# Turning the final recurrence states beside the prompt's scores, and storing the recurrence outputs later in ScalarE's order

## The chip, the cores and the metric

The kernel runs on one core of one Trainium2 chip. The metric is device time in microseconds (us) of that core for one launch. The profiled execution is a separate one with its own time. TensorE is called PE, ScalarE ACT, VectorE DVE, GpSimd POOL; SP is the engine whose queue issues nearly all the DMAs.

## The reference, cut to what matters

One layer of a hybrid backbone over 1024 latent tokens and 128 prompt tokens, width 1024, float32 (products are made exact enough by splitting an operand into a high and a low part, three matmuls for one). In the layer's mixer, one projection feeds attention heads, a gated linear recurrence and a Fourier mixing:

```
xc = dw_conv(xr, conv_w, conv_b)
hf, hf_fin = rg_lru_dir(xc, ..., h0[:, 0], False)   # forward scan
hb, hb_fin = rg_lru_dir(xc, ..., h0[:, 1], True)    # backward scan
lru_out = (hf + hb) * gelu(gr)                      # into the output projection
new_h = stack([hf_fin, hb_fin])                     # final states of the PROMPT, an output (2 x 256)
```

The prompt attends to itself only (128 x 128 scores for 4 heads x 2 maps); the latent tokens attend to themselves and a cached context. The change touches the place where `lru_out` is split and stored, and the place where `new_h` is turned from columns into rows and written out.

## The kernel before, in words

All instructions are issued in an order written out by hand; each engine runs its own in that order, and a DMA waits in SP's queue behind the DMAs ahead of it. The stretch that matters goes from 213 to 350 us of the span:

- **Projection units.** Fourteen 128-column units of the input projection (u0 and u1 during the start, then twelve in a loop over `i`), each 8 k-steps of 9 matmuls (`pu`). After each k-step `tick(1.44)` advances a planner's clock; each planner queue then runs its generator up to that clock. A generator's `yield x` asks to be resumed x later (plain `yield`: the queue's own wait, 0.806 for the four recurrence queues).
- **Recurrence queues** `ql`: two scan generators (one for each direction), one for the gates (`g` matmuls on PE, sigmoids on ACT, L581 and L583), one for the outputs, `lru_outs`. The recurrence has two halves of 128 channels, called channel half 0 and 1 here. `lru_outs` adds the two directions on POOL (L625), multiplies by the gelu gate on DVE (L628, tile `a`), waits by the `yield` that the change edits, and then runs `store_mix` in four parts: high part on ACT (L168; `mh` for half 0, `mor` for half 1), low part on DVE (L174; `ml`, `moi`), two DMAs to `MH` and `ML`.
- **Values, first half.** Nine tiles of 24 matmuls (`v`), with `tick(1.045)` twice for each tile. Their weights are loaded and split before (`load_v(0)`); `load_v(1)` loads `vr` for the second half at the end of the unit loop, splits it into `vwh` on ACT and `vwl` on DVE. Rope of the last query unit (`ry`, `rz`, `ryh`, `ryl`) runs beside it and is written to `QH`, `QL`, `QHP`, `QLP`.
- **`drain_lru()`** then empties the recurrence queues. Last in `lru_outs` before the change is the turn of the states: PE transposes `nh` (L636) into an `aux` PSUM bank ("a"), ACT copies it into a corner of `lw`, SP writes `new_h` (L640).
- **Prompt and values, second half.** `play(PRE)` interleaves, by hand, steps of `prompt_gen` ("p") with k-steps of the second half of the values ("v36" is 36 k-steps of 3 matmuls, using the two `aux` banks in turn, "a" first):

```
    PRE = "p v36 p r p p v6 v4 p v5 l v3 p"
```

  The first "p" issues the six loads of `kp` and `qp`; the second one the sixteen prompt score matmuls (`sp`, L1143, into banks 0 and 1 of a three-bank tile); at "r" the recurrence's memory is released; the third "p" issues `load_q(0, 0)` (four loads `qs`) and `load_head(0)` (two loads `ks`, then `ck`, `av`), which the first scores of the latent tokens need (`s`, L940). Attention then runs to about 525 us, the output projection and the feed-forward part follow.

Of the kernel before, what the change touches and what calls it, by code (L numbers as in the profile page):

```python
# [16 lines left out]
P = 128  # L17
# [135 lines left out]
def _body(tc, nc, A):  # L153
    PE, ACT, DVE, POOL, SP = nc.tensor, nc.scalar, nc.vector, nc.gpsimd, nc.sync
# [6 lines left out]
    def rdma(eng, out, in_):  # L161

        f = lambda v: v.bitcast(F32) if v.dtype == F32R else v
        eng.dma_start(f(out), f(in_))

    def copy(eng, out, in_):
        if eng is ACT:
            ACT.activation(out, in_, AF.Copy)  # L168
        else:
            eng.tensor_copy(out, in_)  # L170
# [31 lines left out]
    ident = cp.tile([P, P], F32, name="ident")  # L202
# [19 lines left out]
    def aux(name, tag):  # L222
        return ax.tile([P, 512], F32, name=name, tag="aux" + tag)
# [212 lines left out]
    def store_mix(stage, k, src, parts=3, full=None):  # L436

        w = T // parts
        for q in range(parts):
            c = slice(q * w, (q + 1) * w)  # L440
            if full is None:
                mh, ml = [stage.tile([P, w], F32R, name=f"m{i}{k}{q}", tag=f"m{i}", bufs=1)
                          for i in "hl"]
            else:
                mh, ml = [x[:, c] for x in full]
            copy(ACT, mh, src[:, c])
            yield
            lo(ml, src[:, c], mh)
            yield
            rdma(SP, MH[k * P:(k + 1) * P, c], mh)  # L450
            rdma(SP, ML[k * P:(k + 1) * P, c], ml)
            yield
            yield
# [94 lines left out]
    xin, ggr, lru = {}, {}, {}  # L548

    def until(*names):  # L550
        while not all(n in lru for n in names):
            yield 0.3
# [66 lines left out]
    def lru_outs(f, lw, nh):  # L619
        for u in range(2):  # L620
            yield from until(("scan", u, 0), ("scan", u, 1))
            yield 2.021
            h, h1 = lru["scan", u, 0][0], lru["scan", u, 1][0]
            o = lru["scan", u, 1][1]
            POOL.tensor_tensor(h, h, h1, op=OP.add)  # L625
            yield 2.64
            for s0, o0, w in ((0, 0, NL), (NL + GAP, NL, NP)):
                DVE.tensor_tensor(o[:, o0:o0 + w], h[:, s0:s0 + w], ggr[u][:, o0:o0 + w],  # L628
                                  op=OP.mult)
            yield 0.994  # L630
            full = ([f.tile([P, TL], F32R, name=f"mo{i}", tag=i, bufs=2) for i in "ri"] if u else None)
            yield from store_mix(f, 4 + u, o, 4, full)
            lru["out", u] = True
        yield from until(*[("fin", u, d) for u in range(2) for d in range(2)])
        b = aux("nht", "a")
        PE.transpose(b[0:4, 0:P], nh.rearrange("p d u -> p (d u)"), ident)  # L636
        yield 4.0
        nhs = lw[0:4, 0, 0, 0]
        copy(ACT, nhs, b[0:4, 0:P])
        SP.dma_start(A["new_h"].rearrange("d (u p) -> (d u) p", p=P), nhs)  # L640


    kq = {}
# [193 lines left out]
    def load_q(h, c):  # L837
        q = kv.tile([P, 2, 2, CW], F32R, name=f"qs{h}{c}", tag="qs", bufs=2)
        hs = slice(h * P, (h + 1) * P)
        for half, (s0, s1) in ((0, (QH, QL)), (1, (QL, QH))):  # L840
            ps_ = slice(64 * half, 64 * half + 64)
            for st_, src in ((0, s0), (1, s1)):
                s = src[hs].rearrange("(m d) t -> d m t", m=2)
                w = min(CW, NL - c * CW)
                rdma(SP, q[ps_, st_, :, :w], s[:, :, c * CW:c * CW + w])
        qsl[h, c] = q
# [62 lines left out]
    def aux_free(name):  # L909

        return aux(name, "ab"[((vdone - 1) // KT + 1) % 2])
# [215 lines left out]
    def prompt_gen():  # L1127

        big = lambda name, tag, dt=F32: aw.tile([P, 9 * P], dt, name=name, tag=tag,
                                                bufs=3 if tag == "wt" else 2)  # L1130
        small = lambda name, w: aw.tile([P, w], F32, name=name, tag=name, bufs=1)
        f = P_["kq"]
        kp, *qp = [f.tile([P, T], F32R, name=n, tag=t, bufs=1)
                   for n, t in (("kp", "ab0"), ("qp0", "ab1"), ("qp1", "rope"))]
        g8 = lambda x: x[:, :8 * P].rearrange("p (g c) -> p g c", c=P)
        for half, ss in ((0, (KHP, QHP, QLP)), (1, (KLP, QLP, QHP))):
            for dst, src in zip((kp, *qp), ss):
                rdma(SP, g8(dst)[64 * half:64 * half + 64], src)
        yield
        b = sc.tile([P, 3, 512], F32, name="sp", tag="s")  # L1140
        for g in range(8):
            for st_ in range(2):
                PE.matmul(b[:, g // 4, g % 4 * P:g % 4 * P + P], g8(qp[st_])[:, g], g8(kp)[:, g],  # L1143
                          start=(st_ == 0), stop=(st_ == 1))
        yield
        nm, ss, c, so = small("nmp", 8), small("ssp", 8), small("cp", 4), small("sop", 4)
        ACT.activation(ss, mhalf[:, :8], AF.Exp)
        load_q(0, 0)
        load_head(0)
        vp = aw.tile([P, CW], F32, name="vp", tag="wth", bufs=6)  # L1150
        SP.dma_start(vp[:, :2 * P], VS[NL:T, 0:2 * P])
        s = b[:, 0:2].rearrange("p a (q c) -> p (a q) c", c=P)
        DVE.tensor_reduce(nm, s, axis=AX.X, op=OP.max, negate=True)
        e = big("ep", "p0")
        for i in range(2):
            yield
            for g in range(4 * i, 4 * i + 4):
                ACT.activation(g8(e)[:, g], s[:, g], AF.Exp, bias=nm[:, g:g + 1],
                               accum_out=ss[:, g:g + 1])
        s0, s1 = ss[:, 0:8:2], ss[:, 1:8:2]  # L1160
        DVE.reciprocal(c, s1)
        DVE.scalar_tensor_tensor(c, c, nlam, s0, op0=OP.mult, op1=OP.mult)
        w, o = big("wtp", "wt"), big("op", "wt")
        hd = lambda x, h: x[:, h * P:(h + 1) * P]
        for h in range(NH):
            DVE.scalar_tensor_tensor(hd(w, h), g8(e)[:, 2 * h + 1], c[:, h:h + 1], g8(e)[:, 2 * h],
                                     op0=OP.mult, op1=OP.add)
        yield
        b = aux_free("tpp")
        for h in range(NH):  # L1170
            PE.transpose(hd(b, h), hd(w, h), ident)
        copy(DVE, o[:, 512:1024], b)
        yield
        b = aux_free("opp")
        for h in range(NH):
            PE.matmul(hd(b, h), hd(o, 4 + h), hd(vp, h) if h < 2 else hd(vst[:, 7], h - 2),
                      start=True, stop=True)
        for h in range(NH):
            ACT.activation(o[:, 1024:], hd(b, h), AF.Square, accum_out=so[:, h:h + 1])
        DVE.scalar_tensor_tensor(c, s0, EPS, s0, op0=OP.mult, op1=OP.mult)  # L1180
        DVE.scalar_tensor_tensor(so, so, 1.0 / P, c, op0=OP.mult, op1=OP.add)
        POOL.tensor_tensor(so, so, mhalf[:, :NH], op=OP.pow)
        yield
        for h in range(NH):
            DVE.tensor_scalar(hd(o, 4 + h), hd(b, h), so[:, h:h + 1], None, op0=OP.mult)
        yield
        b = aux_free("onp")
        for h in range(NH):
            PE.transpose(hd(b, h), hd(o, 4 + h), ident)
        for i in range(2):  # L1190
            x = b[:, 256 * i:256 * i + 256]
            mh, ml = [aw.tile([P, CW], F32R, name=f"mp{i}{a}", tag="wth", bufs=6)[:, :256]
                      for a in "hl"]
            ACT.activation(mh, x, AF.Copy, scale=gsub)
            DVE.scalar_tensor_tensor(ml, x, gsub, mh.bitcast(F32), op0=OP.mult, op1=OP.subtract)
            for dst, t_ in ((MH, mh), (ML, ml)):
                rdma(SP, dst[256 * i:256 * i + 256, NL:T].rearrange("(h p) t -> p h t", p=P),
                     t_.rearrange("p (h t) -> p h t", h=2))
# [24 lines left out]
    for n in range(N + 7):  # L1223
        a, t_, v, c = n, n - 3, n - 4, n - 6
# [23 lines left out]
        if has(a):  # L1248
            U[a] = {}
            h, t = units[a]  # L1250
# [238 lines left out]
    def bank(name):  # L1489
        nonlocal nbank  # L1490
        i = banks[nbank % len(banks)]
        nbank += 1
        pl, tag = (ga, f"g{i}") if i < 4 else (gb, f"g{i}") if i < 6 else (dn, "dn")
        return pl.tile([P, 512], F32, name=name, tag=tag)
# [192 lines left out]
    for i, (n, t) in enumerate(runs):  # L1687
# [5 lines left out]
        b = bank(f"d{n}_{t}")  # L1693
        for j in range(NJ):
# [21 lines left out]
            h = hid[t, j // 11]  # L1716
# [36 lines left out]
```

## Time and profile before

| | us |
|---|---|
| median of 3 runs (lowest, highest) | 1432.75 (1431.6, 1433.61) |
| profiled execution, its time | 1430.3 |
| profiled execution, its span from first to last instruction | 1428.5 |

The 1.8 us between time and span lie outside the first and last instruction. The profile shows single executions: a row gives start, duration, engine, line, operation, output and inputs, and in brackets how long the engine sat idle before it and what ended that. Matmuls of the fp32 kind are recorded as two instructions each (so one gate matmul counts as x2).

### The profile page before, as it was taken

Reading aid. Unit: us, or ns where it says so; the run is one execution under the profiler, and the core shown is the slowest. Engines: PE = TensorE matmul, PEld = TensorE weight load, DVE = VectorE, ACT = ScalarE, POOL = GpSimd, SP = SyncE. Lnnn points to the kernel's source line nnn. Section 1 sums busy time; section 2 is a strip of 40 time slices with the busy share of each in tenths; the row PEclk is TensorE's granted clock in tenths of the full one; section 3 lists DMA queues with packets and bytes.
Section 4 is the critical chain, followed back from the end, with each engine's and each line's share of the span. In section 5 each row is a group of like instructions: output and inputs, shape, how many; then the busy total and the mean of one; then the engine's idle time right before and its main releaser. Section 6 shows DMA issues by size and latency. Waiting matters only on the chain.

```text
span 1428.5 us, 22758 instructions
## 1 busy us (share of the span) xinstructions
PE 1375.9 (96%) x8918; PEld 1248.9 (87%) x8918; DVE 822.0 (58%) x1247; ACT 573.4 (40%) x1138; POOL 427.6 (30%) x426
## 2 busy tenths in 40 slices
PE   7899999998999999998999999999999989999998
PEld 6887799888889888887899999999999968888886
DVE  5724464564888843667866767667666653243232
ACT  6511136734888863555322323223222342142120
POOL 2301111222666662447634334333423100000000
PEclk9999999999999999999999999999999999999999
DMA  8558840147755335563222312222222472334541
GB/s 328 178 202 276 266 158 31 63 158 174 179 136 146 96 108 166 176 209 111 78 93 64 101 59 93 84 74 99 67 77 82 137 275 89 115 109 166 182 151 59
DMA packets 108326, 193.40 MB, mean 135 GB/s; under 512 B 7701, under 2 KB 77754, under 8 KB 104762
## 3 DMA queue, kind: packets, MB, share of 16 engines
q1 hardware_dynamic: 108074, 191.41, 41.7%
q8 instruction: 71, 1.16, 0.4%
q10 hardware_dynamic: 144, 0.52, 0.1%
q14 instruction: 37, 0.30, 0.1%
HBM read 146.67 MB, written 45.24 MB: 134 GB/s over the span
## 4 chain that ended last, share of the span: by engine, by line
PE 49%; DVE 2%; issue 1%; ACT 1%; DMA 1%; POOL 0%; DVEq 0%; POOLq 0%; SPq 0%; ACTq 0%
PE g L186 10%; PE g L184 10%; PE g L185 10%; PE d L186 6%; PE d L184 6%; PE d L185 6%; DVE gu L174 1%; DMA hr<-HB 1%; DVE av L174 0%; ACT gu L168 0%; DMA raw_gu<-in_w_down 0%; DVE u L1530 0%; DVE hf L1530 0%; DVE hd L174 0%; ACT av L168 0%
## 5 line engine op out<-in xcount | busy, mean ns | idle before, releaser
L186 PE MATMUL g<-av,gu 128*128 128x320 f32 (+1 forms) x1232 | 364.2, 296 | 7.7 <-DVE gu L174 7.3
L184 PE MATMUL g<-av,gu 128*128 128x320 f32 (+1 forms) x1232 | 364.3, 296 | 1.2 <-ACT av L168 0.8
L185 PE MATMUL g<-av,gu 128*128 128x320 f32 (+1 forms) x1232 | 363.1, 295 | 0.0
L186 PEld LDWEIGHTS g<-av,gu 128*128 128x128 f32 x1232 | 232.1, 188 | 10.3 <-DVE gu L174 10.2
L184 PEld LDWEIGHTS g<-av,gu 128*128 128x128 f32 x1232 | 231.9, 188 | 2.3 <-issue 1.4
L185 PEld LDWEIGHTS g<-av,gu 128*128 128x128 f32 x1232 | 232.2, 188 | 0.0
L174 DVE TENSOR_TENSOR gu<-raw_gu,gu 128x512 fp32r<-128x512 f32 x139 | 141.2, 1023 | 40.1 <-ACT gu L168 40.1
L184 PE MATMUL pu<-hl,w 128*128 128x384 f32 x336 | 123.0, 366 | 4.6 <-POOL hl L174 3.8
L186 PE MATMUL pu<-hh,w 128*128 128x384 f32 x336 | 113.1, 337 | 0.0
L185 PE MATMUL pu<-hh,w 128*128 128x384 f32 x336 | 113.1, 337 | 0.0
L184 PE MATMUL d<-dw,hd 128*128 128x512 f32 x270 | 106.7, 395 | 3.2 <-DVE dw L174 3.1
L186 PE MATMUL d<-dw,hd 128*128 128x512 f32 x270 | 106.4, 394 | 0.9 <-DVE hd L174 0.9
L185 PE MATMUL d<-dw,hd 128*128 128x512 f32 x270 | 106.4, 394 | 0.0
L1371 POOL TENSOR_TENSOR raw_gu<-raw_gu,t 128x512 f32<-128x512 f32 x25 | 33.2, 1329 | 233.4 <-DVE gu L174 233.4
L1530 DVE TENSOR_TENSOR u<-g,u 128x320 f32<-128x320 f32 (+1 forms) x176 | 77.5, 450 | 29.8 <-PE g L186 29.8
L940 PE MATMUL s<-ks,qs 128*128 128x384 f32 x384 | 91.0, 358 | 3.0 <-ACT p L953 1.5
L946 DVE TENSOR_REDUCE nm<-s 128x1 f32<-128x1152 f32 x64 | 86.6, 1353 | 9.4 <-PE s L940 9.2
L953 ACT ACTIVATE p<-s,nm 128x1152 f32<-128x1152 f32 x64 | 78.2, 1222 | 29.5 <-DVE nm L946 16.4
L1672 ACT ACTIVATE t<-d 128x512 f32<-128x512 f32 x18 | 10.7, 596 | 186.4 <-PE d L186 186.4
L168 ACT ACTIVATE gu<-raw_gu 128x512 fp32r<-128x512 f32 x139 | 83.4, 620 | 3.5 <-DMA raw_gu<-in_w_down 3.4
L1080 POOL TENSOR_SCALAR fv<-fv 128x1 f32<-128x1 f32 x9 | 2.7, 303 | 271.5 <-ACT t L1672 271.5
L184 PEld LDWEIGHTS pu<-hl,w 128*128 128x128 f32 x336 | 63.3, 189 | 21.7 <-issue 14.1
(276 smaller groups left out, 2867.4 us busy)
## 6 DMA issues: line engine op xcount, KB each, us to landing
raw_gu<-in_w_gu SPq DMA_DIRECT2D x25, 1024.0 KB, 4.8
hr<-HB SPq DMA_DIRECT2D x32, 704.0 KB, 5.0
wmb<-in_w_mod SPq DMA_DIRECT2D x32, 512.0 KB, 5.0
raw_gu<-in_w_down SPq DMA_DIRECT2D x22, 512.0 KB, 4.2
HB<-hf SPq DMA_DIRECT2D x18, 576.0 KB, 3.1
x<-in_x SPq DMA_DIRECT2D x18, 512.0 KB, 4.6
wm<-in_w_mod SPq DMA_DIRECT2D x16, 512.0 KB, 7.7
raw<-in_w_in_u SPq DMA_DIRECT2D x14, 512.0 KB, 7.7
```

The costliest lines, as they stand in the source:

```text
L168: ACT.activation(out, in_, AF.Copy)
L174: eng.tensor_tensor(out, x, hi.bitcast(F32), op=OP.subtract)
L184: PE.matmul(out, wh, xl, start=first, stop=False)
L185: PE.matmul(out, wh, xh, start=False, stop=False)
L186: PE.matmul(out, wl, xh, start=False, stop=last)
L940: PE.matmul(b[:, j, :CW], q[:, st_, m, i * P:(i + 1) * P], ks[:, m, j * CW:(j + 1) * CW], start=(st_ == 0), stop=(st_ == 1))
L946: DVE.tensor_reduce(nm, s, axis=AX.XY, op=OP.max, negate=True)
L953: ACT.activation(p.rearrange("p (n c) -> p n c", c=CW), s, AF.Exp, bias=nm, accum_out=ss)
L1080: POOL.tensor_scalar(v[:, 0:1], v[:, 0:1], v[:, 1:2], D * EPS, op0=OP.add, op1=OP.add)
L1371: POOL.tensor_tensor(b21, b21, t2, op=OP.subtract)
L1530: add = lambda out, x: DVE.tensor_tensor(out, b, x, op=OP.add)
L1672: ACT.activation(t2, b, AF.Square, accum_out=fv[:, t, n:n + 1])
```

## The change

The wait between the multiplication and the four store parts becomes 5.0 instead of 0.994 on the planner's clock, for both channel halves. The transpose of the states, its copy and the `new_h` DMA leave the end of `lru_outs`; `lru_outs` only leaves the operands in `lru["state"]`. They are issued in `prompt_gen` instead, right behind the sixteen prompt score matmuls, into the third bank of the same tile, and the copy is made by DVE instead of ACT. The wait of 4.0 and the ACT copy disappear.

```diff
                 DVE.tensor_tensor(o[:, o0:o0 + w], h[:, s0:s0 + w], ggr[u][:, o0:o0 + w],
                                   op=OP.mult)
-            yield 0.994
+            yield 5.0
...
         yield from until(*[("fin", u, d) for u in range(2) for d in range(2)])
-        b = aux("nht", "a")
-        PE.transpose(b[0:4, 0:P], nh.rearrange("p d u -> p (d u)"), ident)
-        yield 4.0
-        nhs = lw[0:4, 0, 0, 0]
-        copy(ACT, nhs, b[0:4, 0:P])
-        SP.dma_start(A["new_h"].rearrange("d (u p) -> (d u) p", p=P), nhs)
+        lru["state"] = nh.rearrange("p d u -> p (d u)"), lw[0:4, 0, 0, 0]
...
                 PE.matmul(b[:, g // 4, g % 4 * P:g % 4 * P + P], g8(qp[st_])[:, g], g8(kp)[:, g],
                           start=(st_ == 0), stop=(st_ == 1))
+        h, hs = lru["state"]
+        PE.transpose(b[0:4, 2, 0:P], h, ident)
+        copy(DVE, hs, b[0:4, 2, 0:P])
+        SP.dma_start(A["new_h"].rearrange("d (u p) -> (d u) p", p=P), hs)
         yield
```

## Rows read from the trace of the kernel before

**Rows 1.** PE's timeline, 260 to 282 us.
```profile
260.16 1.65 PE L581 MATMUL g<-xc,lw 128*128 128x385 f32 x2 [2.60 <-ACT r L583]
...
263.93 1.46 PE L581 MATMUL g<-xc,lw 128*128 128x385 f32 x4
...
266.80 0.81 PE L581 MATMUL g<-xc,lw 128*128 128x385 f32 x2
...
269.01 0.81 PE L581 MATMUL g<-xc,lw 128*128 128x385 f32 x2
...
281.06 0.28 PE L184 MATMUL v<-vwl,hh 128*128 128x256 f32 x1
```

**Rows 2.** ACT's timeline, 259 to 287 us.
```profile
259.19 0.44 ACT L168 ACTIVATE mh<-a 128x288 fp32r<-128x288 f32 x1 [4.55 <-DVE a L628]
...
283.28 1.12 ACT L168 ACTIVATE ab<-pu 128x1152 f32<-128x1152 f32 x1
284.30 1.99 ACT L168 ACTIVATE vwh<-vr 128x1024 fp32r<-128x1024 f32 x2
```

**Rows 3.** PE's timeline, 306 to 311 us.
```profile
306.96 0.27 PE L636 MATMUL nht<-ident,nh 128*4 128x128 f32 x1
310.69 0.39 PE L184 MATMUL v<-vwl,hh 128*128 128x256 f32 x1 [3.46 <-ACT lw L168]
```

**Rows 4.** ACT's timeline, 307 to 316 us.
```profile
307.51 0.68 ACT L675 ACTIVATE ryh<-ry 128x576 fp32r<-128x576 f32 x1 [2.60 <-DVE ry L671]
...
310.39 0.25 ACT L168 ACTIVATE lw<-nht 4x128 f32<-4x128 f32 x1
315.36 0.39 ACT L168 ACTIVATE vst<-v 128x256 f32<-128x256 f32 x1 [4.72 <-PE v L186]
```

**Rows 5.** PE's timeline, 326 to 339 us.
```profile
326.73 2.20 PE L1143 MATMUL sp<-kp,qp 128*128 128x128 f32 x15 [0.75 <-DMA qp<-QHP]
...
338.24 0.94 PE L940 MATMUL s<-ks,qs 128*128 128x384 f32 x4 [1.16 <-DMA ks<-KL]
```

**Rows 6.** SP's timeline, DMA issues, 277 to 329 us (issue start, issue time).
```profile
277.41 0.92 SPq L798 DMA_DIRECT2D vr<-in_w_in_v  x2
...
305.75 0.52 SPq L164 DMA_DIRECT2D QL<-ryl  x1
...
316.44 0.31 SPq L640 DMA_DIRECT2D out_new_h<-lw  x1
316.84 0.52 SPq L164 DMA_DIRECT2D kp<-KHP  x1
...
321.75 2.97 SPq L878 DMA_DIRECT2D VS<-vst  x3
324.77 0.61 SPq L164 DMA_DIRECT2D qs<-QH  x1
...
328.53 0.60 SPq L164 DMA_DIRECT2D ks<-KL  x1
```

**Rows 7.** Busy time by stretch; the last columns are PE's granted clock, DMA share, GB/s.
```profile
322.00:326.00 4.00, 3.69 (x30) 3.37 (x28) 0.00 (x0) 1.88 (x3) 0.00 (x0) 1.00 1.01 219
326.00:328.00 2.00, 1.27 (x12) 1.30 (x12) 0.00 (x0) 0.00 (x0) 0.00 (x0) 1.00 1.14 363
328.00:330.00 2.00, 2.00 (x12) 2.00 (x12) 1.03 (x1) 0.00 (x0) 0.00 (x0) 0.52 0.99 193
```

**Rows 8.** DMA issues, 275 to 290 us (size, median us from issue to landing).
```profile
vr<-in_w_in_v SPq DMA_DIRECT2D x2, 512.0 KB, 4.7
ML<-ml SPq DMA_DIRECT2D x2, 144.0 KB, 1.7
```

**Rows 9.** DMA issues, 375 to 400 us.
```profile
qs<-QH SPq DMA_DIRECT2D x2, 192.0 KB, 4.0
```

**Rows 10.** Where PE sat idle, by group, 330 to 380 us.
```profile
L940 PE MATMUL s<-ks,qs 128*128 128x384 f32 x96 | 22.4, 353 | 3.0 <-ACT p L953 1.5 <-DMA ks<-KL 1.2 <-DVE ks L174 0.4
```

**Rows 11.** Busy time by stretch in attention (columns as in rows 7).
```profile
397.00:406.50 9.50, 9.44 (x74) 9.02 (x73) 7.94 (x14) 8.89 (x22) 7.93 (x8) 1.00 0.29 88
```

## The prediction

> **What bounds the kernel now.** I read the page first, then the waits and each engine's timeline from 230 to 350 us, because the diff touches nothing else; last the DMA views of the same stretch. From 350 us on the attention stretches keep PE busy almost without a gap at the full clock [rows 11], and everything behind them follows in order, so an amount by which the latent tokens' first scores start later or earlier is carried to the end in full. The question is therefore what sets that start.
>
> The change goes for two stalls of PE. The first is at 257.5 us: PE waits 2.60 us for a sigmoid [rows 1], and the sigmoid stands behind `mh`, for which ACT itself waited 4.55 us, until DVE had made `a` [rows 2]. The second is at 307.2 us: PE has turned the states and waits 3.46 us for ACT to copy them out [rows 3], because that copy is the last of a pile that ACT works off after `ryh` [rows 4]. Each also costs clock: the stretch from the gate matmul after the first stall to the next pair takes 3.77 us, where the same work (one gate matmul, nine others) takes 2.21 us between 266.80 and 269.01 [rows 1]. So 1.56 us are lost at the lower of the two levels, 1.2 instead of 2.4 GHz. I take 1.5 for the second stall too, as it is longer. Together 2.60 + 1.56 + 3.46 + 1.5 = 9.1 us.
>
> But look at what PE meets next. Through with its 36 k-steps, it waits from 326.0 to 326.73 for the last `qp` load, and its next wait, from 337.1 to 338.24, is for `ks` [rows 5, 10]. These come from SP: from 305.75 to the last `qp` issue SP hardly pauses, the loads of `kp` and `qp` start at 316.84 behind all stores of rope, values and recurrence, and `qs` and `ks` follow from 324.77 to 329.1 [rows 6]. From 322 on the DMA engines are full, at 219 GB/s [rows 7]. So the start of the scores is set by SP's order and the transfers behind it. PE's two stalls lie ahead of a wait that would have held it anyway.
>
> **The change part by part.** *The longer wait, half 0.* On the planner's clock each of the four store parts comes 4.0 later, about three k-steps. Stepping the queues by hand puts the first part behind five more sigmoids, so ACT no longer stops ahead of them; `a` is then finished before its turn. PE gains 2.60 + 1.56 = 4.16 us. A smaller wait comes up three gate matmuls later, for the sigmoid behind the two activation-table loads, some 0.4 us longer than now. I take 3.8 net: the values start at 277.2 instead of 281.06 [rows 1], and `ab` on ACT at about 278.6 instead of 283.28 [rows 2].
>
> This lead goes no further along ACT. The fourth store part now stands behind the last square on ACT, and its two DMAs stand in SP's queue ahead of the loads of `vr`. I get the `ML` issue at 279.0 and `vr` at 279.4 instead of 277.41 [rows 6]; they land 4.7 us later [rows 8], at 284.1, and `vwh` starts there, against 284.30 now [rows 2]. ACT waits meanwhile. The last square root and rope, behind `vwh` and `vwl`, gain 0.2 to 0.7 us, mostly because DVE's split no longer runs beside POOL.
>
> *The longer wait, half 1.* The same eight DMAs are still all issued ahead of `kp`. Two parts come after the last value copies on ACT. Rope's last chunk is not delayed by a store part and is about 0.4 us sooner. SP's issues are the same in number, but `new_h`, 0.40 us from issue to issue [rows 6], leaves from ahead of `kp`. Sum for the `kp` issue: between 0.4 (only `new_h`) and 1.5 us earlier; I take 0.85 (the 0.40, and 0.45 of rope's 0.2 to 0.7), so 316.0.
>
> *The turn taken out.* The `aux` bank is free at once and PE goes on at about 303.2, runs two tiles, and then waits for ACT's first `vst` copy, which still stands behind the pile that ends at about 310.4 [rows 4]. It reaches the prompt's scores at about 320 and waits there for `qp`, which lands 0.85 us earlier, at about 325.8. PE's own gain ends here: of 9.1 us, 0.85 is left.
>
> *The turn put in.* The scores took 2.20 us at the full clock [rows 5, 7]. Now they follow some 6 us of idleness, where before there were two short gaps. After the 2.60 us wait the slow stretch took 1.7 times as long [rows 1]; that gives 2.2 to 4.4 us, and I take 3.6. The Trainium skill ("TensorE: Matmul & The Clock Gate", "The HAM clock gate") says the throttled state is the array's default and that activity releases it; the slow stretch agrees, and by it alone the scores would take the whole 4.4. They end at 329.5. The transpose costs 0.27 [rows 3]; the copy on DVE is not in the trace, nearest is ACT's copy of the same shape, 0.25 [rows 4]; with the handing over and the issue of `new_h` itself about 1.2 in all (0.8 to 1.6). Nothing hides this on SP: the third "p", with four `qs` and two `ks`, is queued right behind `new_h`. Before, SP stood there waiting for values only [rows 6]. So the first `qs` issues at 330.7 instead of 324.77, 5.9 us later.
>
> How much of it reaches the scores depends on the transfers. Before, the last `ks` landed 13.3 us after the first `qs` issue (324.77 to 338.1), in a full queue [rows 5, 6]. Now the stores of values go out early and the engines drain. 4 x 192 KB and 2 x 512 KB are 1.84 MB: the first load takes about 4.0 us [rows 9], the other 1.64 MB at 219 GB/s 7.5 us, together 11.5; at the 363 GB/s that one stretch shows [rows 7] it would be 8.5. I take 11.0: landing at 341.7, the scores at 341.8, 3.5 us later than 338.24. PE's work between the prompt's scores and these took 8.2 us (328.9 to 337.1) [rows 5], so it is through at about 338, waits 3 to 4 us and starts slow again, costing 0 to 1.6, taken as 0.5.
>
> **Sum.** 3.5 + 0.5 = 4.0 us later, 1430.3 + 4.0 = 1434.3 for a profiled execution. That one lay 2.45 below the median of the runs, so the prediction is 1432.75 + 4.0 = 1436.8 us. Bounds of this case alone: 2.9 to 6.
>
> **The rivals.** *B, the transfers make it up.* If the drained queue delivers in 8.5 us, `ks` lands at 339.2: 1.0 us later, 1433.8. For it: the early `kp` and the emptied queue; against it: most of the stretch moved 193 to 219 GB/s [rows 7]. It decides from about 9.9 us down. A change of up to 2.9 us either way (0.2%) is about what a measurement here can't tell from none.
>
> *C, ScalarE's lead passes through, faster.* If the fourth store part doesn't hold up `vr`, rope and SP's pile move by up to 4 us: `kp` at 312.8, `qp` landed at 322.6, prompt scores done by 324.9, `qs` at 326.1, `ks` at 334.6 with the quick transfers. PE's 8.2 us of work in between end at 333.4, so the latent scores start at 334.7, 3.5 us earlier: 1429.2. It needs the `kp` issue before about 313.5 as well as 8.5 us. Against it: the two DMAs ahead of `vr`. Removing waits would win outright by the Trainium skill's advice to optimise what blocks the matmul engine ("Perfetto Trace Analysis", "Optimization Strategies"). As a mechanism here, that is both stalls gone with nothing late behind them: 1432.75 - 9.1 = 1423.6. The `qp` wait [rows 5] speaks against it.
>
> *D, memory released later.* The recurrence's memory is reused by the attention tiles. If `qs` lies over `lw`, it also waits for `new_h` to land, 1.7 us by the nearest small DMA [rows 8]: 1438.5. If only `ks` does, the four issues ahead cover it.
>
> **How the numbers follow.** A 0.50, B 0.27, C 0.11, the two stalls in full 0.02, D 0.10. Slower is A and D, 0.60; within 0.2% is B, 0.27; faster 0.13. The range leaves out the full gain, most of C and the far end of D: 1431 to 1440.5; A's own is 1435.6 to 1438.8.
>
> **What would show it.** PE without the waits at 257 and 307 us, and instead a wait of about 2 us for a `vst` copy near 309, one of about 6 for `qp` near 320, and one of 4 to 5 for `ks`; `vr` issued later; SP standing several microseconds for DVE ahead of `new_h`; a dip of the DMA share near 330 us; the prompt scores slow. The prediction is wrong if `kp` is issued well before 315, or if `qs` is not queued behind `new_h`, or if `ks` lands under 10 us after the first `qs`.

## The result, and the profile after

| | before | changed |
|---|---|---|
| median of the runs compared (lowest, highest), us | 1432.17 (1430.55, 1433.61), 4 runs | 1445.76 (1443.36, 1448.2), 4 runs |
| profiled execution, its time (span), us | 1430.3 (1428.5) | 1446.22 (1444.4) |

The changed kernel takes 1.0095 times as long, 95% interval 1.0075 to 1.0116. That is 13.6 us (10.7 to 16.6) where 4.0 were forecast, outside the range. It is slower, as forecast, and the loss that was forecast is there; but a second one of about the same size, which the prediction put at nothing, came on top.

The two profiled executions differ by 1.9 us already at the first gate matmul (215.34 against 213.47), far ahead of anything that was changed. All comparisons below are therefore counted from that matmul.

PE's timeline after, at the place of the first stall and further down, answers to [rows 1, 3, 5]:

```profile
259.27 0.81 PE L581 MATMUL g<-xc,lw 128*128 128x385 f32 x2
...
269.56 1.56 PE L581 MATMUL g<-xc,lw 128*128 128x385 f32 x4 [0.60 <-ACT i L583]
...
317.83 0.58 PE L184 MATMUL v<-vwl,hh 128*128 128x256 f32 x1 [3.76 <-ACT vst L168]
...
332.53 0.44 PE L1138 MATMUL sp<-kp,qp 128*128 128x128 f32 x1 [5.93 <-DMA qp<-QLP]
333.64 3.46 PE L1138 MATMUL sp<-kp,qp 128*128 128x128 f32 x15 [0.66 <-DMA qp<-QHP]
336.90 0.41 PE L1141 MATMUL sp<-ident,nh 128*4 128x128 f32 x1
...
349.93 2.37 PE L935 MATMUL s<-ks,qs 128*128 128x384 f32 x6 [3.89 <-DMA ks<-KL]
```

Both stalls of before are gone, and others stand in their place: 3.76 us for the first `vst` copy, 5.93 and 0.66 for `qp`, 3.89 for `ks`. What PE gained at the old places it waits at the new ones.

ACT's timeline after, against [rows 2]:

```profile
263.45 0.43 ACT L168 ACTIVATE mh<-a 128x288 fp32r<-128x288 f32 x1
...
280.36 1.28 ACT L598 ACT_TABLE_LOAD   x1 [4.24 <-DVE th L612]
281.66 1.26 ACT L598 ACTIVATE a<-r,spn 128x1155 f32<-128x1155 f32 x1
...
285.17 0.43 ACT L168 ACTIVATE mh<-a 128x288 fp32r<-128x288 f32 x1
285.50 1.11 ACT L168 ACTIVATE ab<-pu 128x1152 f32<-128x1152 f32 x1
292.01 1.06 ACT L168 ACTIVATE vwh<-vr 128x1024 fp32r<-128x1024 f32 x1 [5.39 <-DMA vr<-in_w_in_v]
```

The end of the scan that this table load waits for, on DVE's timeline after:

```profile
279.89 0.40 DVE L612 TENSOR_TENSOR_SCAN th<-a,i 128x128 f32<-128x128 f32 x1
```

The same place on ACT's timeline before:

```profile
275.52 0.45 ACT L168 ACTIVATE mh<-a 128x288 fp32r<-128x288 f32 x1 [1.09 <-DMA MH<-mh]
...
278.46 1.28 ACT L598 ACT_TABLE_LOAD   x1
279.76 1.27 ACT L598 ACTIVATE a<-r,spn 128x1155 f32<-128x1155 f32 x1
```

The first `mh` no longer waits. But the table load of the last scan's exponential waits 4.24 us for DVE (`th`, L612: the scan before it), a wait that the kernel before doesn't have; there the last `mh` came ahead of the exponential, now it comes behind. Everything behind the wait on ACT is later, the last `mh` at 285.17 too, and `vr`, whose loads stand behind that part's DMAs.

SP's timeline after, against [rows 6]:

```profile
286.12 0.32 SPq L164 DMA_DIRECT2D ML<-ml  x1
286.49 0.94 SPq L793 DMA_DIRECT2D vr<-in_w_in_v  x2
...
323.77 0.52 SPq L164 DMA_DIRECT2D kp<-KHP  x1
...
328.68 1.74 SPq L873 DMA_DIRECT2D VS<-vst  x3
337.66 0.29 SPq L1143 DMA_DIRECT2D out_new_h<-lw  x1
338.01 0.61 SPq L164 DMA_DIRECT2D qs<-QH  x1
...
341.27 0.61 SPq L164 DMA_DIRECT2D ks<-KL  x1
```

SP issues nothing from 330.4 to 337.66, because `new_h` at the head of its queue waits for DVE's copy; `qs` follows at once. Busy time by stretch after (columns as in [rows 7]) shows what this does to the DMA engines, and PE's clock beside it:

```profile
332.00:334.00 2.00, 0.81 (x3) 0.65 (x3) 0.00 (x0) 0.00 (x0) 0.00 (x0) 0.50 1.03 316
334.00:336.00 2.00, 2.00 (x11) 2.00 (x11) 0.00 (x0) 0.00 (x0) 0.00 (x0) 0.50 0.12 39
336.00:338.00 2.00, 2.00 (x12) 2.00 (x12) 0.65 (x2) 0.00 (x0) 0.00 (x0) 0.50 0.00 0
338.00:340.00 2.00, 2.00 (x11) 2.00 (x11) 0.76 (x1) 1.08 (x7) 0.00 (x0) 0.50 0.17 48
340.00:342.00 2.00, 2.00 (x14) 2.00 (x14) 0.00 (x0) 2.00 (x12) 0.00 (x0) 0.66 0.97 247
```

For six microseconds the DMA engines are all but idle, where before they were full [rows 7], and the prompt's scores run at the lower clock level, 0.50.

### The profile page after: what moved, and what is told of

Its sections match the earlier page's. It is cut to its first block, busy times and chain, and to the rows that moved or that the text cites. A ratio compares the mean times of both kernels' runs of the same rounds, so it can differ in the third digit from the quotient of the medians.

```text
span 1444.4 us, 22760 instructions
## 1 busy us (share of the span) xinstructions
PE 1385.2 (96%) x8918; PEld 1257.5 (87%) x8918; DVE 823.6 (57%) x1248; ACT 573.2 (40%) x1137; POOL 426.3 (30%) x426
## 4 chain that ended last, share of the span: by engine, by line
PE 49%; DVE 2%; DMA 1%; issue 1%; ACT 1%; POOL 0%; SPq 0%; DVEq 0%; POOLq 0%; ACTq 0%
PE g L186 10%; PE g L184 10%; PE g L185 10%; PE d L186 6%; PE d L184 6%; PE d L185 6%; DMA hr<-HB 1%; DVE gu L174 1%; DVE av L174 0%; DMA raw_gu<-in_w_down 0%; ACT gu L168 0%; DVE u L1529 0%; ACT hd L168 0%; DVE hd L174 0%; ACT av L168 0%
## 5 line engine op out<-in xcount | busy, mean ns | idle before, releaser
L184 PE MATMUL d<-dw,hd 128*128 128x512 f32 x270 | 107.8, 399 | 3.4 <-DVE dw L174 3.4
L186 PE MATMUL d<-dw,hd 128*128 128x512 f32 x270 | 107.7, 399 | 0.4 <-DVE hd L174 0.4
L185 PE MATMUL d<-dw,hd 128*128 128x512 f32 x270 | 107.5, 398 | 0.0
L1671 ACT ACTIVATE t<-d 128x512 f32<-128x512 f32 x18 | 10.7, 596 | 185.4 <-PE d L186 185.4
```

The source lines that it names most:

```text
L184: PE.matmul(out, wh, xl, start=first, stop=False)
L185: PE.matmul(out, wh, xh, start=False, stop=False)
L186: PE.matmul(out, wl, xh, start=False, stop=last)
L1671: ACT.activation(t2, b, AF.Square, accum_out=fv[:, t, n:n + 1])
```

## The experiments

**Theory 1**, formed from these rows: two losses that add. The later store parts keep the tile `a` of channel half 0 in use, so the last scan's exponential has to wait for the other of the two buffers; and `new_h` blocks SP. **Its main rival:** only one of the two matters. Each run is read at the same marks, starts counted from the kernel's first gate matmul, minus the same in the profile of before. The marks are the `kp` issue, the first `qs` issue, the first latent scores (`s`) and the first matmul of the output projection (`op`). The next two columns are lengths: of the feed-forward stretch from its first `g` to the first `d` matmul, and of the last stage, from the first `d` matmul to the end of the last one. The last column is the timed ratio to before, which was run beside each of them.

| kernel | kp | qs | s | op | g to d, us | d, us | ratio, 95% interval |
|---|---|---|---|---|---|---|---|
| before | 0 | 0 | 0 | 0 | 502.8 | 280.1 | |
| changed | +5.1 | +11.4 | +9.8 | +10.9 | 503.1 | 282.9 | 1.0095 (1.0075, 1.0116) |
| e1 wait only | +5.3 | +5.3 | +5.2 | +5.3 | 503.0 | 279.6 | 1.0038 (1.0018, 1.0057) |
| e2 turn only | +0.2 | +6.3 | +5.6 | +6.9 | 503.1 | 280.6 | 1.0038 (1.0019, 1.0057) |
| e3 other tile | -0.8 | +5.4 | +3.4 | +5.0 | 503.1 | 279.6 | 1.0031 (1.0011, 1.0050) |
| e4 new_h off SP | +4.6 | +4.1 | +5.2 | +4.5 | 500.5 | 278.4 | 0.9992 (0.9974, 1.0009) |
| e5 columns only | +0.5 | +1.4 | +1.0 | +1.9 | 499.2 | 279.0 | 0.9965 (0.9950, 0.9980) |
| e6 both | -0.3 | -0.8 | -0.2 | -0.6 | 500.7 | 277.1 | 0.9957 (0.9938, 0.9977) |
| e7 vr early | -3.9 | -4.3 | -3.6 | -4.5 | 500.5 | 277.9 | 0.9926 (0.9906, 0.9946) |
| e8 queue only | +4.5 | +5.2 | +5.5 | +4.9 | 503.1 | 282.9 | 1.0031 (1.0008, 1.0054) |
| e9 values first | -4.0 | -2.4 | -3.7 | -4.0 | 499.1 | 277.8 | 0.9944 (0.9924, 0.9964) |
| e10 16 bytes | -2.1 | -2.0 | -1.7 | -0.6 | 499.4 | 276.5 | 0.9931 (0.9911, 0.9951) |
| e11 32 bytes | -0.5 | -0.4 | +0.4 | +1.2 | 499.2 | 277.8 | 0.9950 (0.9926, 0.9974) |

e5, e10 and e11 change no order of work in this stretch, and their marks scatter by up to 2 us either way; smaller differences between runs are not read as effects.

**e1: only the longer wait.** The changed kernel without the moved turn.

```diff
-            yield 0.994
+            yield 5.0
```

> Only the wait of 5.0; the turn of the states stays at the end of the recurrence, as before. Theory 1 (the later store parts hold the tile that the last scan's exponential needs, ACT waits some 4 us, and the loads of vr, rope and SP's pile come some 5 us later): 3 to 7 us slower than before, the kp loads issued about 5 us later. Rival (the later store parts do no harm, all of the loss comes from new_h standing in SP's queue ahead of the loads): within 2 us of before, no wait of ACT ahead of the last exponential.

Measured 5.2 to 5.3 us at every mark and 1.0038 in time. ACT's timeline of this run has the new wait, and PE's has the old stall at the turn, longer than before:

```profile
277.96 1.28 ACT L598 ACT_TABLE_LOAD   x1 [4.25 <-DVE th L612]
```

```profile
315.12 0.58 PE L184 MATMUL v<-vwl,hh 128*128 128x256 f32 x1 [9.25 <-ACT lw L168]
```

The rival is out: the longer wait alone costs 5 us. And a stall of 9.25 us at the turn costs nothing beyond it: the marks behind it are no later than `kp`.

**e2: only the turn moved.** The changed kernel with the wait of before.

```diff
-            yield 5.0
+            yield 0.994
```

> Only the turn is moved; the wait stays 0.994. Theory 1 (two separate losses that add): no wait of ACT ahead of the last exponential, kp issued within 0.5 us of before, qs issued 5 to 7 us later than before, the time 4 to 7 us above before. Rival (the turn alone is hidden by the drained DMA queue, as in B of the prediction): within 2 us of before.

`kp` is at its old place, `qs` 6.3 us later, `s` 5.6, `op` 6.9. SP's timeline of this run:

```profile
324.80 1.54 SPq L873 DMA_DIRECT2D VS<-vst  x3
333.56 0.29 SPq L1143 DMA_DIRECT2D out_new_h<-lw  x1
333.90 0.61 SPq L164 DMA_DIRECT2D qs<-QH  x1
```

So both parts cost, and at `op` their 5.3 and 6.9 make 12.2 against 10.9 together: they add, within the scatter of the marks.

**e3: the buffer freed.** The changed kernel; the gated output is written over the backward scan's result, so that `a` is free after its scan.

```diff
-            o = lru["scan", u, 1][1]
+            o = lru["scan", u, 1][0]
```

> The changed kernel, with the gated output of a channel half written into the backward scan's result tile instead of its coefficient tile, so that the coefficient tile is free early. Theory 1: the 4.2 us wait of ACT ahead of the last exponential is gone, vr is issued about 5 us sooner, and the time falls by 4 to 7 us against the changed kernel, to about 1440, which is what the prediction summed without that wait. Rival (that wait lies beside another one, the store parts ahead of vr in SP's queue): under 2 us better than the changed kernel.

ACT's timeline of this run: the table load follows the square root at once, and the last `mh` comes 4 us sooner than in the changed kernel. It reads `th` now.

```profile
275.14 1.17 ACT L605 ACTIVATE th<-th 128x1155 f32<-128x1155 f32 x1
276.33 1.28 ACT L598 ACT_TABLE_LOAD   x1
...
281.14 0.43 ACT L168 ACTIVATE mh<-th 128x288 fp32r<-128x288 f32 x1
...
286.38 2.25 ACT L168 ACTIVATE vwh<-vr 128x1024 fp32r<-128x1024 f32 x2 [3.79 <-DMA vr<-in_w_in_v]
```

With that one tile exchanged the profile shows what the prediction had summed: `kp` 0.8 us sooner (forecast 0.85), `s` 3.4 later (forecast 3.5), `op` 5.0 later (forecast 4.0), and 4.4 us in time (1.6 to 7.2). To a tenth this is luck, as the marks scatter by 2 us, but the wait was the occupied buffer.

**e4: `new_h` off SP.** The changed kernel with three edits: its queue, and the places of the state columns and rows.

```diff
-        nh = f.tile([P, 2, 2], F32, name="nh")
+        nh = nhc
...
+    nhc = cp.tile([P, 2, 2], F32, name="nhc")
...
-        lru["state"] = nh.rearrange("p d u -> p (d u)"), lw[0:4, 0, 0, 0]
+        lru["state"] = nh.rearrange("p d u -> p (d u)"), kq["nk"][0:4, 0:P]
...
-        SP.dma_start(A["new_h"].rearrange("d (u p) -> (d u) p", p=P), hs)
+        ACT.dma_start(A["new_h"].rearrange("d (u p) -> (d u) p", p=P), hs)
```

> The changed kernel, with new_h issued from ACT's queue instead of SP's, and with the state columns in the constants' memory and their rows in the prompt's key staging tile, so that nothing of the attention tiles lies over them. Theory 1: qs is issued some 7 us sooner than in the changed kernel, right behind the stores of values; the first latent scores start 4 to 5 us sooner; the time is 4 to 6 us below the changed kernel, about 1440.5. Rival (the transfers, not SP's order, set the scores): under 2 us better.

`qs` is 7.3 us sooner than in the changed kernel, `s` 4.7, `op` 6.4: the second loss, shown by removing it. The time fell by more than that, to that of before, and the table says where the rest is: the feed-forward stretch is 2.7 us shorter than in the changed kernel and the last stage 4.5, though the edit changes no order of work there. That had to be explained before any time with this edit could be read.

**e5, e10, e11: where the tiles lie.** The kernel before with the state columns among the constants (the first two hunks of e4), or with unused bytes there instead: sixteen for each partition in e10 (shown), thirty-two in e11 (`[P, 8]`).

```diff
+    pad = cp.tile([P, 4], F32, name="pad")
+    POOL.memset(pad, 0.0)
```

> The kernel before, with nothing changed but the 16 bytes of the state columns, which stand among the constants, so that all tiles allocated behind them lie elsewhere. In the run with new_h off SP the feed-forward stretch was some 2.4 us shorter than in every other run, with matmuls 0.5 to 1% closer together. Theory P (that is the place of the tiles): the same shorter feed-forward stretch here, and 2 to 5 us below before. Rival (chance of that chip or run): feed-forward stretch as before, time within 1.5 us.

> The kernel before with 16 unused bytes among the constants (cleared once on POOL), nothing else. Theory P (the place of the tiles behind it shortens the matmuls' spacing): the feed-forward stretch 2 to 4 us shorter than before, the time 2 to 6 us below, as with the state columns there. Rival (it was the state columns' own place): as before within 1.5 us.

> The same with 32 unused bytes. If only the distance from a 32-byte boundary matters, the time and the feed-forward stretch are those of before; if any shift helps, 2 to 6 us below it.

All three are faster than before, by 0.35 to 0.69% (5.0 to 9.9 us, in e10 and e11 more than expected), and all have the short feed-forward stretch. So sixteen or thirty-two bytes that nobody reads are worth up to 9.9 us, where the change cost 13.6. It is not the place of the columns themselves, and not the distance from a 32-byte boundary; what the three have in common is that the tiles allocated behind lie elsewhere. The whole feed-forward stretch, of the kernel before and of e10 (columns as in [rows 7]):

```profile
639.10:1141.90 502.80, 493.96 (x3707) 490.19 (x3706) 346.89 (x529) 159.27 (x310) 193.56 (x141) 1.00 0.27 89
```

```profile
640.60:1140.00 499.40, 490.08 (x3707) 486.46 (x3706) 346.60 (x529) 158.95 (x310) 195.11 (x141) 1.00 0.26 89
```

The same 3707 matmul records, at the same granted clock, take 3.4 us less, so the clock is not the cause. Why a shift does this stays open; how far the tiles moved, and which tile of which engine it concerns, was not tried. The last stage is shorter too, 276.5 to 279.0 us in the seven kernels with something added among the constants, against 279.6 to 280.6 in before, e1, e2 and e3. The times of e4, e6, e7 and e9 contain this gain; their marks up to `op` show none beyond the scatter.

**e6: both cures.** e3's edit and e4's.

> The changed kernel with both cures: the gated output in the other tile, and new_h off SP's queue with the state columns in the constants' memory. Theory 1: kp issued 0.5 to 1 us sooner than before counted from the gates, qs right behind the stores of values, the first latent scores within 1.5 us of before; the output projection starts 4 to 5 us sooner than with the other tile alone. Time, counting the shorter feed-forward part: 2 to 5 us below before. Rival (the two losses overlap): no better than with new_h off SP alone, which was 0.8 parts in a thousand below before.

All marks are within 1 us of before. With the two causes taken out, nothing of the loss is left, and nothing is gained either, as the prediction's accounting says: PE's two stalls were worth nothing while SP and the transfers set the scores. In time e6 is 6.2 us below before, a little more than expected, and that is again the place of the tiles as far as the marks tell.

**e7: `vr` early.** e6, and the loads of `vr` in the last projection unit, ahead of the last store parts.

```diff
             if i == NU - 2 and k == 4:
                 load_v(0)
+            if i == NU - 1 and k == 2:
+                load_vr(1)
             tick(1.44)
```

The diff is cut to the call: `load_vr` holds the two DMAs of `load_v`, which skips them when they have been issued.

> As the run with both cures, and the loads of vr for the second half of the values issued in the last projection unit, ahead of the last store parts. Theory 1, with the prediction's rival C (ScalarE's lead passes through once vr doesn't hold it): vwh starts about 4 us sooner, kp is issued 3 to 5 us sooner than before counted from the gates, the first latent scores 2 to 5 us sooner; 2 to 4 us below the run with both cures. Rival (SP's pile of stores holds kp anyway): kp within 1.5 us of before, no gain over the run with both cures.

ACT's timeline of this run:

```profile
284.33 1.11 ACT L168 ACTIVATE ab<-pu 128x1152 f32<-128x1152 f32 x1
285.34 1.99 ACT L168 ACTIVATE vwh<-vr 128x1024 fp32r<-128x1024 f32 x2
```

`vwh` starts right behind `ab`, without the wait, 66.9 us after the first gate matmul (285.34 - 218.45) where it was 70.8 before (284.30 - 213.47). `kp`, `s` and `op` come 3.6 to 4.5 us sooner than before. That is the prediction's rival C (`kp` 4.0 sooner, the scores 3.5), once its condition and both cures are supplied. The kernel takes 0.9926 of before. Against e6, whose tiles have the same addition, `op` comes 4.0 us sooner, and that is the order of work; the rest fits the place of the tiles, and by time alone e7 can't be told from e10.

**e8: only the queue.** The changed kernel with only the last hunk of e4.

> The changed kernel with new_h issued from ACT's queue and nothing else; the state columns and rows stay in the recurrence's memory. Theory D (the prediction's last rival: attention tiles lie over that memory and wait for new_h to land): qs issues right behind the stores of values, but ks waits for new_h, so that ks issues within 2 us of the changed kernel and the time stays within 2.5 us of it. Rival (nothing lies over it): ks issues 5 to 6 us sooner, the time 4 us or more below the changed kernel, with the feed-forward stretch as in before.

The load `ks<-KL` issues 5.4 us sooner than in the changed kernel (5.5 us later than before, against 10.9), so nothing of `qs` or `ks` lies over the states, and rival D is out. SP's timeline of this run shows `av` waiting instead, from 336.60 to 343.66, which e4's doesn't do (`av` at 337.43 there, right behind `ck`), and the waits of SP's queue say for what:

```profile
336.01 0.59 SPq L827 DMA_DIRECT2D ck<-in_cache_kt  x1
343.66 0.38 SPq L828 DMA_DIRECT2D av<-VS  x1
```

```profile
SPq L828 <- DMA out_new_h<-lw: 7.0, 1, 7.0
```

So reused memory does hold a load up, but one that is needed later. The feed-forward stretch is 503.1, and the marks are within 1.1 us of e4's: the two edits of memory in e4 gave the place, the queue gave the order.

**e9: values first.** e7 with eight k-steps moved ahead of the prompt's scores.

```diff
-    PRE = "p v36 p r p p v6 v4 p v5 l v3 p"
+    PRE = "p v44 p r p p v2 p v5 l v3 p"
```

> As the run with vr early, with eight k-steps of the values moved from behind the prompt's scores to ahead of them, into PE's wait for qp. Theory T (the transfers behind SP's order set the latent scores, PE only waits in another place): PE's wait for qp shrinks by about 3 us and a wait for ks of 1 to 3 us appears ahead of the latent scores; the time stays within 2 us of the run with vr early. Rival (in that kernel PE's work behind the prompt's scores sets them): no wait for ks, 2.5 to 3 us faster than it.

No gain: `s` at -3.7 instead of -3.6, `op` at -4.0 instead of -4.5. PE's timeline of this run:

```profile
324.74 4.04 PE L1151 MATMUL sp<-kp,qp 128*128 128x128 f32 x16 [3.60 <-issue]
335.44 1.03 PE L1183 MATMUL tpp<-ident,wtp 128*128 128x128 f32 x4 [0.91 <-DVE wtp L1178]
336.83 0.94 PE L948 MATMUL s<-ks,qs 128*128 128x384 f32 x4 [0.37 <-DMA ks<-KL]
338.16 0.63 PE L948 MATMUL s<-ks,qs 128*128 128x384 f32 x2 [0.39 <-DVE ks L174]
```

The waits only moved. Ahead of the prompt's scores PE stands 3.60 us, for which this profile names no cause, where it waited 6.5 for `qp` in e7; and waits for `wtp`, `ks` and its split appear around the first latent scores, where e7 has none. The wait for `ks` is shorter than the 1 to 3 us expected, because a wait for the prompt's own chain (0.91) comes ahead of it; PE's work and the transfers end within a microsecond of each other here.

## Why the prediction had one loss right and missed the other

The step that failed is in "The longer wait, half 0": *"I get the `ML` issue at 279.0 and `vr` at 279.4"*. It moved the fourth store part behind the last square on ACT, and let that square, and the exponential ahead of it, run as soon as ACT was free; a wait for the tile that the exponential writes was put at nothing. But the store parts read `a`, there are two buffers of `a` (`bufs=2`), and in the new order the last store part comes behind the exponential that writes the fourth `a` (on ACT 285.17 against 281.66; before 275.52 against 279.76). So that exponential takes the buffer of the third `a`, which is free only when DVE has scanned it, at 280.29: a wait of 4.24 us in the changed kernel, 4.25 in e1, none in e3. Counted from the first gate matmul, `vr` was issued 7.2 us later than before, not 2.0; without the wait, in e3, 2.9. The forecast "0.85 us earlier" for `kp` became 5.1 later, and that error of 5.9 us is most of the 9.6 by which the time was missed.

The other terms, with the rows of the changed kernel:

- The first stall goes, and a wait of 0.60 us follows where there was one of 0.27. The values start 4.2 us sooner, 3.8 forecast.
- PE's lead ends in waits: 3.76 us for `vst` (about 2 forecast), 6.6 for `qp` (about 6), 3.89 for `ks` (4 to 5).
- The prompt's scores run at the lower level: 15 of them in 3.46 us instead of 2.20; 3.6 forecast for the sixteen. The prediction read the 2.20 as the full clock, but [rows 7] have 0.52 from 328 on, so their last 0.8 us were slow already. 1.4 us at the full level and 0.8 at half of it make 1.8 us of full-clock work, and twice that is 3.6, near the 3.46.
- The Trainium skill's rule ("TensorE: Matmul & The Clock Gate", "The HAM clock gate") agrees with the trace: 0.50 is granted from 331.1, within the wait of 5.93 us, and full speed comes back after PE has worked again, by 341.3. The 4.4 that the prediction worked out by it was too much, because it doubled the whole 2.20.
- From the scores' end (337.10) to the first `qs` (338.01) 0.91 us, 1.2 forecast.
- From the first `qs` to the latent scores 11.9 us, 11.0 forecast; the 8.5 of rival B didn't come, though the DMA engines had drained. The first 2 us after the pause move only 48 GB/s.
- PE's slow restart: 1.1 us between `s` and `op` in the changed kernel, 1.6 in e3, where 0.5 was taken and 1.6 was the bound. In the changed kernel the granted clock is 0.50 from 348.2 to 355.0, over the start of the latent scores; in e1 and e6, where it is back at 1.00 by 336.3 and 340.3, ahead of them, nothing is lost between the two marks (0.0 and -0.4).

Of the rivals, C needed further edits to come true (e7), and D was wrong about the tile. The two stalls were what blocked PE, and both were removed; the time rose, and in e6 it bought nothing. The Trainium skill's advice ("Perfetto Trace Analysis", "Optimization Strategies") is to optimise the engines that are "blocking the critical path", and the two stalls were not on it: the `qp` wait behind them would have held PE anyway.

Up to `op` the changed kernel's profile is 10.9 us behind, at its end 14.0. Of what is lost behind `op`, 2.8 us lie in the last stage, and the granted clock shows how: it is 0.50 for 6.8 us from 1174.2, after a wait of 2.17 us for the weights `dw`. PE's row at the end of that wait, and the busy time of 3.4 us of the slow stretch (columns as in [rows 7]):

```profile
1173.07 0.50 PE L184 MATMUL d<-dw,hd 128*128 128x512 f32 x1 [2.17 <-DVE dw L174]
```

```profile
1177.60:1181.00 3.40, 3.40 (x10) 2.63 (x9) 1.62 (x1) 0.74 (x3) 0.00 (x0) 0.50 0.94 349
```

In the kernel before, the same place of the last stage runs at the full level:

```profile
1164.50:1168.00 3.50, 3.50 (x17) 2.92 (x16) 1.83 (x2) 0.05 (x1) 0.00 (x0) 1.00 1.03 419
```

So the 10.0 us by which this profile misses the forecast of 4.0 are 5.9 for the buffer (changed against e3 at `op`), 1.0 of e3 against the forecast, 0.3 in the feed-forward stretch and 2.8 in the last stage. e8 has the same there (0.50 for 6.8 us, after a wait of 2.20), and before, e1, e2 and e3 have no slow stretch. No edit changes the order of work in that stage; whether the wait comes with the change or by chance stays open, and the interval of the timed difference, 10.7 to 16.6 us, holds 11 as well as 14.

## What to carry to other kernels

Moving a consumer later in an engine's order lengthens the life of what it reads: before doing it, list the buffers it reads, how many there are, and which instruction next needs one. Before removing a stall, find the next wait of the same engine and ask what sets its end; if that is a queue elsewhere, the stall costs nothing by itself (e6) and only the queue is worth work (e7). And an output that nobody waits for should not be issued on the queue that carries the next stage's loads, unless its producer is surely done by then.

## What was not expected of the hardware

Sixteen or thirty-two unused bytes among the constants shorten a feed-forward stretch of 502.8 us, in which PE is busy for 494.0, to 499.2 to 499.4 us at the same granted clock, and the whole kernel by 0.5 to 0.69%. In the seven kernels with something added among the constants that stretch, whose work is the same, takes 499.1 to 500.7 us, and in the six without it 502.8 to 503.1.
